# HGRN projections as pairs of channel tiles over both token halves, with the residual stream held in DRAM

## The chip, the cores and the metric

The kernel runs on one core of one Trainium2 chip. The metric is device time in microseconds (us), the median of several executions. A core has TensorE (PE in the profile, with PEld for its weight loads), VectorE (DVE), ScalarE (ACT), GpSimd (POOL) and SyncE (SP), which issues all of this kernel's DMAs.

## The reference, cut to what matters

A trunk of two layers over 1024 tokens of width 1024. Each layer is a token mixer and a gated convolutional FFN, each after an RMS norm with a shift and a scale, each added to the residual stream x. Layer 0 mixes with a chunked gMLP, layer 1 with HGRN2, a gated linear recurrence:

```python
q, fz, i, g = jnp.split(h @ w_in, 4, axis=-1)      # four projections, 1024 x 1024 each
f = lb + (1.0 - lb) * jax.nn.sigmoid(fz)
k = 1.0 - f
q = jax.nn.silu(q)
o = hgrn2_chunked_scan(q, k, i, log(f))            # 8 heads of 128 channels
o = o * lax.rsqrt(jnp.mean(o * o, axis=-1, keepdims=True) + EPS) * gn_g
return (o * jax.nn.silu(g)) @ w_out
```

Everything is float32. A product of two float32 matrices is made of three matmuls in a reduced float32 format: each operand is split into a high part and the remainder (low part), and high x high, high x low and low x high are summed (mm3, L268 to L272).

## The kernel before, in words

x is held transposed in SBUF (xT: 128 partitions, 8 channel tiles, 1024 tokens), and all work goes by two token halves of 512, LO and HI. Operations are not issued as they are written: each is given to a planner (class Plan) with its engine, an assumed duration, what it reads and writes and a priority `pr`; the planner schedules them by list scheduling, in its model port=True steps of DVE and POOL exclude each other, and the order that it finds is then the order of the program on each engine.

Both up projections of the FFN, and the gMLP's, use `class Pairs`. A pair is two channel tiles of weights (r = 0, 1) times two halves of tokens. It is computed as a 2 x 2 block product with the weights' channels split in an upper and a lower half of k-tiles (TOP and the rest), in seven products where the plain form has eight. Per pair, `pair` forms four sums of weight blocks (p_comb, L480), splits seven weight operands (p_split: the high half on ACT, L470; the low half on DVE or POOL, L473), runs seven products of 4 k-tiles x 3 matmuls of 512 columns, copies three products from PSUM (snap, ACT, L698) and adds four (add, DVE, L701). The token side needs operands that are made once: `combos` builds, per k-tile of TOP, the sums of the four blocks of h and splits them into T1, T2, T3 and T4 (L646 for the shifted sums). `plain_pair` computes a pair in eight products.

The HGRN stage of layer 1 follows the first FFN. Its norm (p_sum, p_stats, ln_p) gives h in high and low parts for each half, first LO, then HI, whose last steps come behind the down projection's last products; the scaled x of the norm goes to a ring of tiles (tring). Then 16 units, head by half (u = 2 x head + half):

- `project`: three projections (f, q, g) of one head for one half, each 8 k-tiles x 3 matmuls of 512 columns (h_proj, weights stationary), then the gates: sigmoid and scale on ACT, 1 - f (L1434), the silu products (L1444, L1451) and the product with f (L1446) on DVE.
- `iproj`: the values i, token tiles stationary, for two heads at a time: 4 x 8 tiles x 8 k-tiles x 3 matmuls of 256 columns. So the values come out by token and need no transpose.
- `scan`: seven levels (1, 2, ... 64 tokens). Each level multiplies keys and queries (L1487), multiplies halves of keys, queries and decays by decays on DVE (L1493, L1514), copies the others on ACT (L1497) and puts masked scores into place (L1470, L1531). Then the keys are transposed (L1549), the state is updated (L1556, L1565, L1567), the output computed (L1576, L1578), normalised (L1582, the root, L1590) and transposed (L1598), multiplied with the gate (L1600) and stored to DRAM as operands of the output projection (store, L1619).

Weights of a head come as 1024-wide tiles by DMA (L484), are split by ACT and POOL (h_weight), and each unit's projections are written next to the scan of the unit before.

The output projection (block_out) runs seven block products P1, P2, P6, P7, P4, P5, P3 over the stored operands and adds into xT (p_evac, L412). P1 needs only the first halves of the even heads, P2 the first halves of the odd heads, P6 and later products everything. Its weights and operands are loaded and split as buffers come free (L473 with n as output). The second FFN follows with two plain pairs, its combos and twenty pairs.

Of the kernel before, what the change touches and what calls it, by code (L numbers as in the profile page):

```python
# [7 lines left out]
F32 = mybir.dt.float32  # L8
F32R = mybir.dt.float32r
# [4 lines left out]
P = 128  # L14
# [224 lines left out]
def trunk(tc, a, pool, psum, dram):  # L239
# [20 lines left out]
    acts = dram.tile([NPAIR // 2, 7, P, HT], F32, name="act")  # L260
    hacts = dram.tile([NH // 2, 7, P, HT], F32, name="hact")
# [108 lines left out]
    def bv(i, o=0, n=512):  # L370
        return View(bankl[i], o, n)
# [232 lines left out]
    class Pairs:  # L604
# [32 lines left out]
        def combos(self, k, pr, t1=None):  # L637
# [15 lines left out]
            for i, (n, t) in enumerate((("T2", a22), ("T1", s1), ("T3", a12), ("T4", a21))):  # L653
                if n != "T1" or t1 is None:
                    p_split(pl, t, *self.b[n][k], "V", pr + 0.1 * i)

        def product(self, j, i, slot, fine):
            _, bn, bank_, more = self.PRODUCTS[i]
            pl, pr = self.pl, self.base + 7 * j + i
            ps = bv((4 * j + self.b0 + bank_) % 8)  # L660
# [12 lines left out]
        def pair(self, j, fine=False):  # L673
# [3 lines left out]
            def p(i):  # L677
                return self.base + 7 * j + i
# [640 lines left out]
    tring = Seq(*(v for c in nc_[0:2] for v in two(c, F32)))  # L1319
# [38 lines left out]
    hcell = [hc[i] for i in (6, 0, 3, 5, 8, 1, 11, 10, 4, 7, 9, 2)]  # L1358
    sigs = Seq(*parts(hcell[0], 512, 512))
    f_a, f_b = parts(hcell[1], 512, 512)  # L1360
    q1, k1 = parts(hcell[2], 512, 512)
    qx, = parts(hcell[3], 768)
    sc_a, = parts(hcell[4], 512)
    fs = Seq(f_a)
    scs = Seq(sc_a, f_b)
    sgs = Seq(*parts(hcell[5], 512, 512))
    vts = Seq(*(parts(hcell[i], 1024)[0] for i in (6, 7, 8)))
    ots = Seq(*parts(hcell[9], 512, 512))
    gos = Seq(*(v for i in (10, 11) for v in parts(hcell[i], 512, 512)))
    t23 = rv(2, 0, 512), rv(2, 512, 512)  # L1370
    pjs, lvs, mis = Seq(0, 1, 2), Seq(3, 4), Seq(5, 6, 7)
    lbc, omc = lbt[:, 3 * KT:4 * KT], lbt[:, 4 * KT:5 * KT]
    p_load(pl, masks, a["masks"], HB - 20)
    hw, vtok, gout = {}, {}, {}

    def h_weight(key, src, pr):
        x = wraw.next()
        hw[key] = hi, lo = wsets.next()
        p_load(pl, x, src, pr)
        p_split(pl, x, hi, lo, "G", pr)  # L1380
# [3 lines left out]

    def iproj(m, tb, pr):
        hf = tb // 4
        if tb % 4 == 0:
            vtok[m, hf] = vts.next()
        b, vt = bv(mis.next(), 0, 256), sub(vtok[m, hf], tb % 4 * 256, 256)
        ts_ = slice(tb * P, tb * P + P)  # L1390
        for q in range(2):
            ws = hw["i", m, q]
            xs = [hop2(4 * q + k, ts_) for k in range(4)]

            def fn(ws=ws, xs=xs, q=q):
                hi, lo = (w.r.rearrange("p (k f) -> p k f", f=256) for w in ws)
                for k, (xh, xl) in enumerate(xs):
                    mm3(b.f, (xh.r, xl.r), (hi[:, k, :], lo[:, k, :]), q == 0 and k == 0, q == 1 and k == 3)
            pl.op("PE", 1.45, fn, r=(*ws, *(v for x in xs for v in x)), w=(b,), pr=pr)
        pl.op("S", 0.4, lambda: S.activation(vt.f, b.f, AF.Copy), r=(b,), w=(vt,), pr=pr)  # L1400

    def h_proj(u, n, pr):
        h, hs = u // 2, halves[u % 2]
        hi, lo = hw[n, h]
        b = bv(pjs.next())
        for k0 in range(0, KT, 2):
            xs = [hop2(k, hs) for k in (k0, k0 + 1)]

            def fn(k0=k0, xs=xs):
                for k, (xh, xl) in enumerate(xs, k0):  # L1410
                    c = slice(k * P, (k + 1) * P)
                    mm3(b.f, (hi.r[:, c], lo.r[:, c]), (xh.r, xl.r), k == 0, k == KT - 1)
            pl.op("PE", 1.362, fn, r=(hi, lo, *(v for x in xs for v in x)), w=(b,), pr=pr)
        return b

    class Unit:
# [3 lines left out]
        def project(self, pr):  # L1420
            h = self.h

            def op(eng, dur, fn, r, w, port=False):
                pl.op(eng, dur, fn, r=r, w=w, pr=pr, port=port)

            def gate(b):
                s_ = sigs.next()
                op("S", 0.6, lambda: S.activation(s_.f, b.f, AF.Sigmoid), (b,), (s_,))
                return s_
            s_ = gate(h_proj(self.u, "f", pr))  # L1430
            f, kk = fs.next(), k1
            op("S", 0.79, lambda: S.activation(f.f, s_.f, AF.Identity, scale=omc[:, h:h + 1], bias=lbc[:, h:h + 1]),
               (s_,), (f,))
            op("V", 0.43, lambda: V.tensor_scalar(out=kk.f, in0=f.f, scalar1=-1.0, scalar2=1.0, op0=ALU.mult, op1=ALU.add),  # L1434
               (f,), (kk,), True)
            b = h_proj(self.u, "q", pr)
            s_q = gate(b)

# [15 lines left out]
        def scan(self, pr, prev, lvs, mis):

            u, h, hf = self.u, self.h, self.hf
            sc = scs.next()
# [79 lines left out]
            v = vtok[h // 2, hf]  # L1537

            def vc(c):
                o = c * 256 + h % 2 * P  # L1540
                return v.f[:, o:o + P]

            def cs(c):
                return slice(c * P, (c + 1) * P)
# [45 lines left out]
            op("V", 0.7, lambda: V.tensor_tensor(out=o.f.rearrange("p (c f) -> p c f", f=P),  # L1590
                                                 in0=b3.f.rearrange("p (c f) -> p c f", f=P),
                                                 in1=r.unsqueeze(2).to_broadcast([P, 4, P]), op=ALU.mult),
               (b3, ("small1", 0, 16)), (o,))
# [27 lines left out]

    units = [Unit(u) for u in range(nu)]
    prev = None
    for u in range(-1, nu):

        pr = HB + 10 * u + 5
        if u == -1:
            for n in "fqg":
                h_weight((n, 0), a["hg" + n][0], pr - 15)
            for q in range(2):  # L1630
                h_weight(("i", 0, q), a["hgi"][0, q], pr - 12)
        if u >= 0:
            prev = units[u].scan(HB + 10 * u, prev, *((lvs, mis) if u < nu - 2 else (Seq(2, 3),) * 2))
        if u + 1 < nu:
            if u + 1 == nu - 1:
                pjs = Seq(0, 1)
            units[u + 1].project(pr)
        if u == -1:
            for tb in range(8):
                iproj(0, tb, pr + 1 + 10 * (tb // 4))  # L1640
        m = (u + 3) // 4
        if u >= 1 and m < NH // 2:
            i = (u + 3) % 4
            for tb in range(2 * i, 2 * i + 2):
# [11 lines left out]
    held = [v.life.cell for n in "fqg" for v in hw[n, NH - 1]]  # L1656
    free6 = [c for c in wc if c not in held]
# [129 lines left out]
def _lay_out(inp):  # L1787
# [37 lines left out]
    out["hgi"] = hw[:, 2 * D:3 * D].reshape(2, 4, P, 4, 256).transpose(3, 0, 2, 1, 4).reshape(4, 2, P, 1024)  # L1825
# [24 lines left out]
```

## Time and profile before

| | |
|---|---|
| median of 3 runs | 2450.69 us (2450.42 to 2450.77) |
| the profiled execution's own time | 2449.32 us |
| its span, first to last instruction | 2447.5 us |
| PE / PEld busy | 2411.3 / 2025.4 us |
| DVE / ACT / POOL busy | 1987.3 / 1199.3 / 473.3 us |
| granted TensorE clock, mean | 0.996 |

Times in a view are counted from the span's start. A group row has the line, engine, operation, output and inputs by the program's names, the shapes and the count; behind the first bar the busy time and the mean of one in ns, behind the second the idle time of the engine just before, and what ended it. A window row has its bounds and length, then the busy time of each engine (x instructions), the granted clock, the DMA engines' share and GB/s. A timeline row has start, duration, engine, line and operation, and in brackets the idle time before it. A wait row has who waited for whom, the total, the number and the longest. A DMA row has the count, the size and the median time from issue to landing. A matmul's own duration overlaps its neighbours', so rates are taken from runs of many.

### The profile page before, as it was taken

What the parts mean: (1) busy time and instruction counts of PE and PEld (TensorE: products, weight loads), DVE (VectorE), ACT (ScalarE), POOL (GpSimd) and SP (SyncE); (2) the same over time, 40 slices, a digit from 0 to 9 for tenths busy, and PEclk for the clock granted to TensorE, in tenths of its full rate; (3) what the DMA queues carried; (4) which work ended last, traced back from release to release, by engine and by line L of the source; (5) the groups of instructions that cost most, each with busy time, mean ns of one, the idle gap of its engine ahead of it and who ended that gap; (6) DMA issues with size and microseconds to landing.
All of it is one profiled execution on the core that took longest, in us unless ns stands there. A gap on an engine that the chain in (4) does not pass through costs nothing.

```text
span 2447.5 us, 33499 instructions
## 1 busy us (share of the span) xinstructions
PE 2411.3 (99%) x11870; PEld 2025.4 (83%) x11870; DVE 1987.3 (81%) x3176; ACT 1199.3 (49%) x2066; POOL 473.3 (19%) x289
## 2 busy tenths in 40 slices
PE   9999999999999999999999999999999999999998
PEld 7888788888788888888889898888777888888886
DVE  8888988898999888977846565657999989989756
ACT  5324665455555554445534444435455555554444
POOL 0222111222222221013211111100222222220121
PEclk9999999999999999999999999999999999999999
DMA  9897669720333324734111111123302332338333
GB/s 357 278 358 263 205 226 323 240 89 24 124 96 123 114 86 166 247 114 120 47 48 35 65 36 57 44 74 108 99 26 87 121 121 92 107 114 299 95 102 97
DMA packets 156266, 331.99 MB, mean 136 GB/s; under 512 B 15681, under 2 KB 34497, under 8 KB 156098
## 3 DMA queue, kind: packets, MB, share of 16 engines
q1 hardware_dynamic: 156098, 329.86, 40.5%
q8 instruction: 93, 1.52, 0.3%
q14 instruction: 75, 0.61, 0.1%
HBM read 254.82 MB, written 74.97 MB: 135 GB/s over the span
## 4 chain that ended last, share of the span: by engine, by line
PE 91%; DVE 4%; DMA 3%; ACT 1%; issue 1%; SPq 0%; DVEq 0%; ACTq 0%
PE pb L272 84%; PE pb L1487 3%; PE pb L1219 1%; DVE h L473 1%; PE pb L1556 1%; PE pb L1576 1%; PE pb L1578 0%; DMA xT<-vd 0%; DVE h L280 0%; PE pb L343 0%; DVE n L473 0%; DMA h<-in_ada 0%; DVE w L473 0%; PE pb L1549 0%; DMA w<-in_down 0%
## 5 line engine op out<-in xcount | busy, mean ns | idle before, releaser
L272 PE MATMUL pb<-h,w 128*128 128x512 f32 (+1 forms) x4212 | 977.6, 389 | 7.7 <-DVE h L473 2.5
L272 PE MATMUL pb<-n,w 128*128 128x512 f32 x3936 | 951.1, 393 | 8.0 <-DVE n L473 3.4
L272 PEld LDWEIGHTS pb<-h,w 128*128 128x128 f32 x4212 | 785.5, 188 | 175.2 <-DVE h L473 5.0
L272 PEld LDWEIGHTS pb<-n,w 128*128 128x128 f32 x3936 | 729.9, 188 | 160.8 <-DVE n L473 5.4
L473 POOL TENSOR_TENSOR w<-w,w 128x512 fp32r<-128x512 f32 x158 | 249.6, 1586 | 862.6 <-ACT w L470 761.4
L470 ACT ACTIVATE w<-w 128x512 fp32r<-128x512 f32 x384 | 237.1, 627 | 245.8 <-PE pb L272 144.4
L272 PE MATMUL pb<-w,n 128*128 128x512 f32 (+1 forms) x1536 | 272.5, 337 | 3.7 <-DVE n L458 3.4
L856 DVE SCALAR_TENSOR_TENSOR raw<-wk,prm,raw 128x1024 f32<-128x1024 f32 x168 | 267.4, 1602 | 5.4 <-ACT raw L852 4.2
L272 PEld LDWEIGHTS pb<-w,n 128*128 128x128 f32 x1536 | 238.3, 190 | 36.1 <-DVE n L458 3.9
L473 POOL TENSOR_TENSOR w<-raw,w 128x1024 fp32r<-128x1024 f32 (+1 forms) x48 | 115.2, 2409 | 529.0 <-ACT w L470 450.5
L473 DVE TENSOR_TENSOR w<-w,w 128x512 fp32r<-128x512 f32 x226 | 161.2, 718 | 40.1 <-ACT w L470 39.4
L470 ACT ACTIVATE w<-n 128x512 fp32r<-128x512 f32 x136 | 85.9, 632 | 173.3 <-PE pb L272 163.1
L698 ACT ACTIVATE wk<-pb 128x512 f32<-128x512 f32 x160 | 94.7, 593 | 136.6 <-PE pb L272 115.1
L473 DVE TENSOR_TENSOR w<-n,w 128x512 fp32r<-128x512 f32 x136 | 100.8, 744 | 60.1 <-ACT w L470 59.7
L701 DVE TENSOR_TENSOR wk<-pb,wk 128x512 f32<-128x512 f32 x160 | 108.4, 687 | 45.7 <-PE pb L272 41.2
L470 ACT ACTIVATE h<-h 128x512 fp32r<-128x512 f32 x198 | 122.1, 617 | 15.9 <-DVE h L473 5.8
L473 POOL TENSOR_TENSOR h<-h,h 128x512 fp32r<-128x512 f32 x48 | 67.9, 1416 | 256.0 <-ACT h L470 245.1
L852 ACT ACTIVATE raw<-wk,prm 128x1024 f32<-128x1024 f32 x84 | 103.6, 1240 | 26.0 <-DVE raw L480 11.5
L1493 DVE TENSOR_TENSOR wk<-wk 128x256 f32<-128x256 f32 x192 | 98.0, 534 | 21.8 <-PE pb L1487 11.1
L473 DVE TENSOR_TENSOR h<-h,h 128x512 fp32r<-128x512 f32 x150 | 109.4, 732 | 5.0 <-ACT h L470 5.0
L1497 ACT ACTIVATE wk<-wk 128x256 f32<-128x256 f32 x192 | 75.6, 417 | 77.1 <-PE pb L1487 61.9
L280 DVE SCALAR_TENSOR_TENSOR h<-h,raw 128x1024 f32<-128x1024 f32 x81 | 103.5, 1305 | 1.5 <-DMA h<-in_ada 1.5
(221 smaller groups left out, 2414.9 us busy)
## 6 DMA issues: line engine op xcount, KB each, us to landing
w<-in_up SPq DMA_DIRECT2D x88, 512.0 KB, 3.7
h<-in_ada SPq DMA_DIRECT2D x81, 512.0 KB, 5.8
act<-raw SPq DMA_DIRECT2D x154, 256.0 KB, 2.3
h<-act SPq DMA_DIRECT2D x124, 256.0 KB, 2.7
n<-in_down SPq DMA_DIRECT2D x64, 256.0 KB, 5.4
h<-gact SPq DMA_DIRECT2D x56, 256.0 KB, 4.0
gact<-xT SPq DMA_DIRECT2D x52, 256.0 KB, 3.7
vd<-h SPq DMA_DIRECT2D x32, 256.0 KB, 4.5
```

What stands on the lines that cost most here:

```text
L272: PE.matmul(ps, L[i // 2], R[i % 2], start=first and i == 0 and not more, stop=last and i == 2, skip_group_check=more)
L280: V.scalar_tensor_tensor(out=raw, in0=raw, scalar=1.0, in1=condr, op0=ALU.mult, op1=ALU.mult, accum_out=mod[:, m:m + 1])
L470: pl.op("S", 0.2 + 0.43 * w, lambda: S.activation(hi.r, src.f, AF.Copy), r=(src,), w=(hi,), pr=pr)
L473: lambda: e.tensor_tensor(out=lo.r, in0=src.f, in1=hi.f, op=ALU.subtract), *preds,
L698: pl.op("S", 0.6, lambda: S.activation(c.f, ps.f, AF.Copy), r=(ps,), w=(c,), pr=p(i) - 10)
L701: pl.op("V", 0.69, lambda: V.tensor_tensor(out=c.f, in0=ps.f, in1=c.f, op=ALU.add), r=(ps, c), w=(c,), pr=p(i) - 8)
L852: pl.op("S", 1.22, lambda: S.activation(y.f, wk[:, o + PADW:o + PADW + T], AF.Identity, bias=pc("conv_b", l * NUP + b), scale=cw(2)), r=(c ...
L856: pl.op("V", 1.26, lambda w=w: V.scalar_tensor_tensor(out=y.f, in0=wk[:, o + w:o + w + T], scalar=cw(w), in1=y.f, op0=ALU.mult, op1=ALU.ad ...
L1219: PE.matmul(ps.f[:, i * P:(i + 1) * P], v.f[:, i * P:(i + 1) * P], wsT[:, j, :], start=True, stop=True)
L1487: PE.matmul(ps_()[0:m, c, :], K.f[:, c * P:c * P + m], q, start=True, stop=True)
L1493: V.tensor_tensor(out=halves_(X2, s)[:, :, i, :], in0=halves_(X, s)[:, :, i, :], in1=pair2()[:, :, o].unsqueeze(2).to_broadcast([P, 256 // ...
L1497: S.activation(halves_(X2, s)[:, :, i, :], halves_(X, s)[:, :, i, :], AF.Copy)
```

## The change

The f, q, i and g projections go over to Pairs, in a new class HgUp. Pair j = 2 x head holds f and q, pair 2 x head + 1 holds i and g, each for both token halves. The first two pairs are plain (eight products, `plain`), the other fourteen have seven. i now comes out by channel, so `done` transposes it by head and half (four 128 x 128 transposes and a copy). `combos` of the HGRN stage's h runs at unit 0; T1 and T3 are split late, since their places hold h and the plain pairs' weights until then. `prepare` replaces `project`; 1 - f and the scaling of the head's output go to ACT.

The pairs keep seven slots of split weights and four more operands than before, so the residual stream leaves SBUF meanwhile: each block of xT is stored to xspill once it is final, the norm writes its scaled x over it, and during the units xT's place holds values, gates, transposed keys, scores and outputs. At the end 16 loads bring it back. The second half of the norm has all its low parts on DVE, where half of them were on POOL. The cells that the output projection and the second FFN use are those of the first FFN in another order.

The core of the diff:

```diff
+    xspill = dram.tile([P, KT, T], F32, name="xs")
...
-        def combos(self, k, pr, t1=None):
+        def combos(self, k, pr, t1=None, late=()):
...
-                if n != "T1" or t1 is None:
+                if n not in late and (n != "T1" or t1 is None):
...
+    def spill(hf, ds, pr):
+        for d in ds:
+            pl.op("D", 0.73, lambda d=d: nc.sync.dma_start(xspill[:, d, halves[hf]], xT[:, d, halves[hf]]),
+                  r=(xrg(d, halves[hf]),), w=(("xs", 2 * d + hf, 2 * d + hf + 1),), pr=pr)
...
-        ln_p(nms[0], 1, 0, rbv[0], lambda d: tring.next(), lambda d: pr + 20 + d)
+        spill(0, range(KT), pr)
+        ln_p(nms[0], 1, 0, rbv[0], lambda d: xv(d, LO), lambda d: pr + 20 + d)
...
+            spill(1, (d,), at() - 4)
...
-        ln_p(nms[1], 1, 0, rbv[1], lambda d: tring.next(), lambda d: at() + d, "VG")
+        ln_p(nms[1], 1, 0, rbv[1], lambda d: xv(d, HI), lambda d: at() + d)
...
+    sc0, scs = rv(2, 512, 512), Seq(xv(6, HI), xv(7, HI))
+    ots = Seq(xv(4, LO), xv(5, LO))
+    gos = Seq(xv(6, LO), xv(7, LO), xv(2, HI), xv(3, HI))
+    hslots = [fr[9], fr[10], fr[11], hc[7], hc[9], hc[2], hc[8]]
+    vg = [[xv(0, HI), xv(4, HI), xv(1, HI), xv(5, HI)], [xv(d, LO) for d in TOP]]
...
+    class HgUp(Pairs):
+        def __init__(self):
+            self.pl, self.l, self.sub, self.base = pl, 1, 0, HB
+            self.slots = Seq(*(two(c, F32R) for c in hslots))
+            self.early = Seq(*(two(c, F32R) for c in fr[0:8]))
+            self.banks = Seq(0, 1, 2)
+            self.t = {k: ((xv(k, LO), xv(k + 4, LO)), (xv(k, HI), xv(k + 4, HI))) for k in TOP}
+            self.bc = [x for y in zip([hc[1], hc[11], hc[3], fr[8]], fr[4:8], fr[0:4]) for x in y]
+            self.sides()
+        def at(self, j, i):
+            return self.base + 10 * (j - 1) + 1 + i * 9 / 7
+        def bankof(self, j, i):
+            return (0, 1, 0, 1, 0, 1, 0)[i] if j == nu - 1 else (0, 1, 0, 2, 0, 2, 1)[i]
+        def raw(self, j):
+            return rv(0), rv(1), rv(2, 0, 512)
+        def weights(self, j):
+            return [a[("hgf", "hgq", "hgi", "hgg")[2 * (j % 2) + i]][j // 2] for i in range(2)]
+        def done(self, j, r, hf, pr):
+            x, h = self.places(j)[2 * r + hf], j // 2
...
+            elif j % 2 and r == 0:
+                b = bv(mis.next())
+                def fn():
+                    for c in range(4):
+                        PE.transpose(b.f[:, cs(c)], x.f[:, cs(c)], ident)
+                pl.op("PE", 0.5, fn, r=(x,), w=(b,), pr=pr)
+                pl.op("S", 0.6, lambda: S.activation(x.f, b.f, AF.Copy), r=(b,), w=(x,), pr=pr)
...
-            op("V", 0.43, lambda: V.tensor_scalar(out=kk.f, in0=f.f, scalar1=-1.0, scalar2=1.0, op0=ALU.mult, op1=ALU.add),
-               (f,), (kk,), True)
+            op("S", 0.6, lambda: S.activation(k1.f, f.f, AF.Identity, scale=-1.0, bias=ones[:, 0:1]), (f,), (k1,))
...
-            op("V", 0.7, lambda: V.tensor_tensor(out=o.f.rearrange("p (c f) -> p c f", f=P),
-                                                 in0=b3.f.rearrange("p (c f) -> p c f", f=P),
-                                                 in1=r.unsqueeze(2).to_broadcast([P, 4, P]), op=ALU.mult),
-               (b3, ("small1", 0, 16)), (o,))
+            def scaled():
+                for c in range(4):
+                    S.activation(o.f[:, cs(c)], b3.f[:, cs(c)], AF.Copy, scale=r[:, c:c + 1])
+            op("S", 1.3, scaled, (b3, ("small1", 0, 16)), (o,))
...
+    up = HgUp()
+    up.start()
+    up.plain(0, (HB - 15, HB - 5))
     units = [Unit(u) for u in range(nu)]
     prev = None
+    for u in range(nu):
+        units[u].prepare(HB + 10 * u - 5)
+        if u == 0:
+            for k in TOP:
+                up.combos(k, HB + 1 + 0.5 * k, late=("T1", "T3"))
+            up.plain(1, (HB - 14, HB + 5))
+            for n, i in (("T1", 0), ("T3", 1)):
+                for k in TOP:
+                    p_split(pl, up.t[k][i][0], *up.b[n][k], "V", HB + 3 + 0.5 * k)
+        if u and u % 2 == 0:
+            up.pair(u + 1)
+        prev = units[u].scan(HB + 10 * u, prev, *((lvs, mis) if u < nu - 2 else (Seq(2, 3),) * 2))
+        if u % 2 and u + 1 < nu:
+            up.pair(u + 1)
+    for hf, ds in ((0, TOP), (1, range(KT)), (0, range(4, KT))):
+        for d in ds:
+            p_load(pl, xv(d, halves[hf]), xspill[:, d, halves[hf]], HB + 10 * nu - 1, r=(("xs", 2 * d + hf, 2 * d + hf + 1),))
...
-    held = [v.life.cell for n in "fqg" for v in hw[n, NH - 1]]
-    free6 = [c for c in wc if c not in held]
+    free6, held = [fr[i] for i in (8, 11, 7, 4, 5, 6)], [fr[i] for i in (0, 1, 2, 3, 9, 10)]
```

More of the change, by code (lines that the diff above doesn't have):

```diff
@@ L1318, in trunk, with xv @@
     nc_ = bc[10:11] + bc[2::3]
-    tring = Seq(*(v for c in nc_[0:2] for v in two(c, F32)))
+    xf = xT.rearrange("p k t -> p (k t)")
+    xl = Life("x", KT * T, ap=xf)
+    def xv(d, hs):
+        return View(xl, d * T + hs.start, HT)
+    def spill(hf, ds, pr):
+        for d in ds:
+            pl.op("D", 0.73, lambda d=d: nc.sync.dma_start(xspill[:, d, halves[hf]], xT[:, d, halves[hf]]),
+                  r=(xrg(d, halves[hf]),), w=(("xs", 2 * d + hf, 2 * d + hf + 1),), pr=pr)
     sqs2 = Seq(*two(nc_[2], F32))
@@ L1370, in trunk @@
-    t23 = rv(2, 0, 512), rv(2, 512, 512)
-    pjs, lvs, mis = Seq(0, 1, 2), Seq(3, 4), Seq(5, 6, 7)
+    fr = f0.freed
+    fqp = [parts(hc[i], 512, 512) for i in (10, 4)]
+    sigs = Seq(*parts(hc[0], 512, 512))
+    q1, k1 = parts(hc[6], 512, 512)
+    qx, = parts(hc[5], 768)
+    sc0, scs = rv(2, 512, 512), Seq(xv(6, HI), xv(7, HI))
+    ots = Seq(xv(4, LO), xv(5, LO))
+    gos = Seq(xv(6, LO), xv(7, LO), xv(2, HI), xv(3, HI))
+    hslots = [fr[9], fr[10], fr[11], hc[7], hc[9], hc[2], hc[8]]
@@ L1372, in trunk, with vgs @@
+    vg = [[xv(0, HI), xv(4, HI), xv(1, HI), xv(5, HI)], [xv(d, LO) for d in TOP]]
+    (v0, g0), vg7 = parts(hslots[6], 512, 512), [v for c in hslots[0:2] for v in parts(c, 512, 512)]
+    def vgs(h):
+        return [v0, vg[0][1], g0, vg[0][3]] if h == 0 else vg7 if h == NH - 1 else vg[h % 2]
+    lvs, mis = Seq(3, 4), Seq(5, 6, 7)
     lbc, omc = lbt[:, 3 * KT:4 * KT], lbt[:, 4 * KT:5 * KT]
     p_load(pl, masks, a["masks"], HB - 20)
[L1374 to L1380, printed above, removed]
+    gout = {}
@@ new lines, in cs, with at, bankof, places @@
+    def cs(c):
+        return slice(c * P, (c + 1) * P)
+    class HgUp(Pairs):
[7 more added lines that the diff above has]
+            self.sides()
+        def at(self, j, i):
+            return self.base + 10 * (j - 1) + 1 + i * 9 / 7
+        def bankof(self, j, i):
+            return (0, 1, 0, 1, 0, 1, 0)[i] if j == nu - 1 else (0, 1, 0, 2, 0, 2, 1)[i]
[3 more added lines that the diff above has]
+            return [a[("hgf", "hgq", "hgi", "hgg")[2 * (j % 2) + i]][j // 2] for i in range(2)]
+        def places(self, j):
+            return vgs(j // 2) if j % 2 else [*fqp[0], *fqp[1]]
+        def done(self, j, r, hf, pr):
+            x, h = self.places(j)[2 * r + hf], j // 2
+            if j % 2 == 0 and r == 0:
+                pl.op("S", 0.6, lambda: S.activation(x.f, x.f, AF.Sigmoid), r=(x,), w=(x,), pr=pr)
+                pl.op("S", 0.79, lambda: S.activation(x.f, x.f, AF.Identity, scale=omc[:, h:h + 1], bias=lbc[:, h:h + 1]),
+                      r=(x,), w=(x,), pr=pr)
+            elif j % 2 and r == 0:
[5 more added lines that the diff above has]
+                pl.op("S", 0.6, lambda: S.activation(x.f, b.f, AF.Copy), r=(b,), w=(x,), pr=pr)
+            elif j % 2:
+                s_ = sigs.next()
+                pl.op("S", 0.6, lambda: S.activation(s_.f, x.f, AF.Sigmoid), r=(x,), w=(s_,), pr=pr)
+                pl.op("V", 0.7, lambda: V.tensor_tensor(out=x.f, in0=x.f, in1=s_.f, op=ALU.mult), r=(x, s_), w=(x,),
+                      pr=pr, port=True)
+        def plain(self, j, prs):
+            for x, w in zip(self.raw(j), self.weights(j)):
+                p_load(pl, x, w, prs[0] - 15)
+            ws = {}
+            for r in range(2):
+                for c in range(2):
+                    ws[r, c] = self.early.next()
+                    p_split(pl, rv(r, 512 * c, 512), *ws[r, c], "G", prs[0] - 15)
+            for hf, hs in enumerate(halves):
+                for r in range(2):
+                    b, c_ = bv(self.banks.next()), self.places(j)[2 * r + hf]
+                    for k0 in range(0, KT, 2):
+                        hi, lo = ws[r, k0 // 4]
+                        xs = [hop2(k, hs) for k in (k0, k0 + 1)]
+                        def fn(k0=k0, hi=hi, lo=lo, xs=xs, b=b):
+                            for k, (xh, xl) in enumerate(xs, k0):
+                                c = slice(k % 4 * P, (k % 4 + 1) * P)
+                                mm3(b.f, (hi.r[:, c], lo.r[:, c]), (xh.r, xl.r), k == 0, k == KT - 1)
+                        pl.op("PE", 1.362, fn, r=(hi, lo, *(v for x in xs for v in x)), w=(b,), pr=prs[hf])
+                    pl.op("S", 0.6, lambda c_=c_, b=b: S.activation(c_.f, b.f, AF.Copy), r=(b,), w=(c_,), pr=prs[hf] - 10)
+                    self.done(j, r, hf, prs[hf])
@@ L1382, in sub @@
     def sub(v, o, n):
         return View(v.life, v.o + o, n)
[L1385 to L1414, printed above, removed]
@@ L1535, in scan @@
                 K, Q, T_ = K2, Q2, T2
-            v = vtok[h // 2, hf]
+            v = self.v
             def vc(c):
[L1540 to L1544, printed above, removed]
+                return v.f[:, cs(c)]
             b1, kT = bv(mis.next()), ots.next()
@@ L1824, in _lay_out @@
     out["hgq"], out["hgf"], out["hgg"] = stat(hw[:, 0:D]), stat(hw[:, D:2 * D]), stat(hw[:, 3 * D:])
[L1825 removed]
+    out["hgi"] = stat(hw[:, 2 * D:3 * D])
     out["ho"] = f["hg_w_out"][0].reshape(NH, P, D)
```

87 lines of the change are left out of this document (18 added, 69 removed).

## The prediction

> **What bounds the kernel now.** I read the page first, then one line's summary to get the length of the stage that is changed, then busy times by window, then the groups by line for prices.
>
> ```profile
> span 2447.5 us, 33499 instructions
> PE 2411.3 (99%) x11870; PEld 2025.4 (83%) x11870; DVE 1987.3 (81%) x3176; ACT 1199.3 (49%) x2066; POOL 473.3 (19%) x289
> PE   9999999999999999999999999999999999999998
> DVE  8888988898999888977846565657999989989756
> PE 91%; DVE 4%; DMA 3%; ACT 1%; issue 1%; SPq 0%; DVEq 0%; ACTq 0%
> ```
>
> TensorE is busy in every slice and holds 91% of the chain that ended last. VectorE (DVE) has room in one place, the slices with 4 to 6 tenths: the HGRN stage, the only one that the change touches.
>
> ```profile
> L1487 PE MATMUL pb<-h,h x128: 216/275/276, 1224.7 to 1699.2; 128*128 128x64 f32 x128
> ```
>
> These are the first matmuls of each of the 16 scan units (head by token half). Their first and last starts give the period: (1699.2 - 1224.7) / 15 = 31.64 us a unit.
>
> ```profile
> core 0: us, PE busy (x) PEld busy (x) DVE busy (x) ACT busy (x) POOL busy (x), PEclk, DMA share, GB/s
> 757.00:975.00 218.00, 218.00 (x963) 180.60 (x962) 194.52 (x223) 112.45 (x162) 50.09 (x32) 1.00 0.35 118
> 1224.70:1240.00 15.30, 15.30 (x100) 13.44 (x99) 7.90 (x20) 7.32 (x17) 1.35 (x1) 1.00 0.01 2
> 1240.00:1256.30 16.30, 16.30 (x111) 15.09 (x111) 2.94 (x6) 4.48 (x8) 6.00 (x3) 1.00 0.31 98
> 1256.30:1667.60 411.30, 410.62 (x2698) 367.42 (x2697) 253.07 (x655) 172.86 (x371) 55.64 (x23) 1.00 0.15 50
> 1699.20:1730.00 30.80, 30.64 (x178) 25.71 (x178) 28.38 (x62) 12.76 (x28) 1.29 (x1) 1.00 0.46 151
> 1699.20:1745.00 45.80, 43.50 (x233) 36.07 (x233) 42.48 (x81) 19.54 (x39) 8.99 (x6) 1.00 0.45 139
> ```
>
> The long row is 13 units: PE 410.62 of 411.30 us, so the stage is bound by PE; per unit DVE works 253.07/13 = 19.5 us (idle 12.2), ACT 13.3, POOL 4.3. The first row is the FFN's up projection, which already works in the form the change brings here (pairs, seven products): PE without a gap, with DVE at 194.52/218 = 89%. The granted clock is 1.00 in each of these rows.
>
> **PE: what the change saves.**
>
> ```profile
> 1149.79 45.04 PE L272 MATMUL pb<-h,w 128*128 128x512 f32 x198
> 1213.17 11.68 PE L272 MATMUL pb<-w,n 128*128 128x256 f32 x96
> L272 PE MATMUL pb<-w,n 128*128 128x256 f32 x768 | 96.2, 284 | 0.0
> L1549 PE MATMUL pb<-prm,wk 128*128 128x128 f32 x64 | 9.7, 274 | 0.7 <-DVE wk L1493 0.7
> ```
>
> Back to back a 512-wide matmul takes 45.04/198 = 0.2275 us, a 256-wide one 11.68/96 = 0.1217 us. Removed: the f, q and g projections, 16 units x 3 x 8 k-tiles x 3 = 1152 matmuls, 262.1 us, and the 768 narrow ones of the i projection, 93.5 us; together 355.6. Added: two plain pairs of 96 and fourteen pairs of 7 products x 4 k-tiles x 3 = 84, so 192 + 1176 = 1368 matmuls, 311.2 us; and 16 groups of four transposes for the values, which are of the kind of L1549 (16 groups, 9.7 us). PE loses 355.6 - 320.9 = 34.7 us of work. By unit: 72 x 0.2275 + 48 x 0.1217 = 22.2 us before, 84 x 0.2275 + 0.6 = 19.7 after, so the period that PE allows falls from 31.64 to 29.1 us.
>
> [...]
>
> **DVE, ACT and POOL: what the pairs cost.**
>
> ```profile
> L480 DVE TENSOR_TENSOR w<-w,w 128x512 f32<-128x512 f32 x96 | 72.4, 756 | 0.9 <-DMA w<-in_down 0.7
> L473 DVE TENSOR_TENSOR w<-w,w 128x512 fp32r<-128x512 f32 x226 | 161.2, 718 | 40.1 <-ACT w L470 39.4
> L701 DVE TENSOR_TENSOR wk<-pb,wk 128x512 f32<-128x512 f32 x160 | 108.4, 687 | 45.7 <-PE pb L272 41.2
> L1434 DVE TENSOR_SCALAR h<-h 128x512 f32<-128x512 f32 x16 | 6.7, 421 | 13.3 <-ACT h L1432 13.3
> L1590 DVE TENSOR_TENSOR h<-pb,small 128x512 f32<-128x512 f32 x16 | 10.9, 682 | 0.0
> L473 POOL TENSOR_TENSOR w<-w,w 128x512 fp32r<-128x512 f32 x158 | 249.6, 1586 | 862.6 <-ACT w L470 761.4
> L470 ACT ACTIVATE w<-w 128x512 fp32r<-128x512 f32 x384 | 237.1, 627 | 245.8 <-PE pb L272 144.4
> L646 DVE SCALAR_TENSOR_TENSOR h<-h,mod,h 128x512 f32<-128x512 f32 x12 | 9.9, 828 | 0.0
> ```
>
> One pair per unit puts on DVE four block sums, four low halves and four additions from PSUM: 4 x 0.756 + 4 x 0.718 + 4 x 0.687 = 8.6 us. Two DVE steps of each unit go to ACT (1 - f, and the scaling of the output): 0.421 + 0.682 = 1.1 us off. DVE has 19.5 + 8.6 - 1.1 = 27.0 us a unit, 93% of 29.1. POOL's three splits make 3 x 1.586 = 4.8 us where it had 4.3. ACT gets seven high halves, three snapshots, the value copy, 1 - f and four short scalings; at 0.627 us for each, and with nothing taken off for what leaves, that is 16 x 0.627 = 10.0, so 23.3 us at most, which is no bound.
>
> Does a scan, which is a chain between DVE, PE and ACT, let DVE be filled to 93%? The window 1699.2 to 1730.0 is the last unit with the next stage's work beside it: DVE is busy 28.38 of 30.80 us, idle 2.4. With that idle time the unit takes 27.0 + 2.4 = 29.4 us, 0.3 over PE's 29.1: **14 x 0.3 = 4 us given back**. Bounds: nothing, if DVE keeps ahead of PE, and the 3.3 us of idle time that DVE has per 30.3 us in the FFN window, which is a rival below. Below nothing is excluded, for PE's count is fixed.
>
> **The start.** Both token halves must be there in full before T2, T3, T4 can be built: per k-tile one block sum, three shifted sums and four low halves, 4 x (0.756 + 3 x 0.828 + 4 x 0.718) = 24.4 us of DVE that was not there, and the four low halves of the second norm that leave POOL (at most 4 x 0.83 = 3.3 us, as the shifted sums, which are of their kind). With the first pair's 4 x 0.756 + 4 x 0.718 = 5.9 that is 33.6 us. Cover: in the two windows from 1224.7 to 1256.3 DVE has 31.6 - 7.90 - 2.94 = 20.8 us idle. Up to 13 us of DVE are left over. PE meanwhile has the second half of both plain pairs (96 x 0.2275 = 21.8 us), products 1 and 2 of the first pair, and the first scan. The FFN has the same changeover from plain pairs to pairs twice:
>
> ```profile
> 600.00:640.00 40.00, 37.95 (x165) 30.46 (x164) 35.38 (x47) 20.31 (x31) 11.83 (x7) 1.00 0.30 99
> 1766.00:1810.00 44.00, 41.48 (x185) 33.02 (x184) 40.55 (x74) 21.05 (x34) 10.85 (x5) 1.00 0.11 36
> 1810.00:1862.00 52.00, 48.34 (x202) 38.17 (x200) 50.01 (x60) 31.31 (x48) 14.80 (x7) 0.97 0.12 39
> ```
>
> PE is idle 2.0 us in the first, 2.5 + 3.7 = 6.2 in the second. I take their mean, **4 us**, with 0 and 13 as ends; a gain is excluded, since PE had no idle time there.
>
> **Holding x in DRAM and getting it back.**
>
> ```profile
> act<-raw SPq DMA_DIRECT2D x154, 256.0 KB, 2.3
> h<-act SPq DMA_DIRECT2D x124, 256.0 KB, 2.7
> gact<-xT SPq DMA_DIRECT2D x52, 256.0 KB, 3.7
> 1194.88 0.75 DVE L412 SCALAR_TENSOR_TENSOR xT<-pb,mod,xT 128x512 f32<-128x512 f32 x1 [1.26 <-PE pb L272]
> 1206.74 1.12 PE L343 MATMUL pb<-h,ones 128*128 128x512 f32 x2
> 1734.33 32.71 PE L272 MATMUL pb<-n,n 128*128 128x512 f32 x143 [2.13 <-DVE n L473]
> ```
>
> The 16 spills go out by SP and land in about 3.7 us; the norm's scaled x, which now overwrites x, waits for them. For the first half the last two products of the down projection hide that; for the second, the last block of x is added at 1194.88 and the broadcast that the norm needs starts at 1206.74, 11.9 us later. I cost it at nothing; without that cover it is 3.7 us, and behind the waiting DVE step would stand the whole second-half norm. On SP the spills stand among the weight loads, which wait until POOL's splits free the raw buffers: one such split, 1.6 us, is the price if a spill is caught behind one, and the cover holds that too.
>
> The 16 reloads stand on SP at the end. Most places are free a unit or more early. x[2] and x[3] of the second half hold the last heads' outputs: after the last combination a store (2.3) and a load (about 2.7) must land before product P2 of the output projection can be added into x, and the addition stands in DVE's queue ahead of the splits for P6. Product P1 has a second new wait: its weights are loaded where T3 lay, and its operand buffers are the first half's h, so it can begin only after the last pair; before, it filled the last scan's gaps. Then the scaling on ACT lengthens the last chain by about 1 us. At present PE loses 45.80 - 43.50 = 2.3 us from 1699.2 to 1745, nearly all in the 2.13 of the row above. I take **3 us**; ends are -1, for a part of those 2.3 could be filled, and 10, the store and the load twice over, when DVE stands still for both.
>
> **The sum** against the profiled execution (2449.32 us, of which the span is 2447.5): -34.7 + 4 + 4 + 3 = -23.7, so 2425.6; the median of the runs shown is 1.4 above that execution: **2427.0 us**. Its own range is 2415 (nothing given back in the unit or at the start, -1 at the end) to 2436 (start 8, end 6, units 6).
>
> **The rivals.**
> - DVE cannot be filled beyond the FFN's 89%. Then the unit takes 27.0/0.892 = 30.3 us, 1.2 over PE's: 14 x 1.2 = 16 in place of 4, and the total is -34.7 + 16 + 7 = -12, **2439**. For it: PE and DVE here wait for each other at each of seven levels, in the FFN hardly. Against it: the 92% of the window at 1699.2.
> - The seams cost their upper ends: 13 at the start, 10 at the end, units 4: -34.7 + 27 = -8, **2443**. For it: 33.6 us of new DVE work against 20.8 idle. Against it: both FFN changeovers, which had DVE at 88 to 96% and lost 2 to 6.
> - The other side: the scan's waits stay, and the pairs come on top of them. DVE's steps start in the program's order; where an addition waits for its product, the scan step behind it waits too, and where a scan step waits for PE, so does the split behind it.
>
> ```profile
> DVE h L1470 <- PE pb L1487: 45.8, 26, 5.3
> DVE small L1582 <- ACT h L1580: 22.0, 13, 3.4
> ```
>
>   These waits in the 13 units are a part of DVE's 12.2 us of idle time a unit. It decides at 31.64 - 27.0 = 4.6 us: if more than that stays, the unit is longer than before. If half stays, 6.1, the unit takes 33.1 us: -34.7 + 14 x (33.1 - 29.1) + 7 = +28, **2479**. Against it: the idle time is there because DVE had nothing else, and it fell to 2.4 where it had.
>
>   [...] No row here shows a ready step held behind a waiting one.
>
> **How the numbers follow.** The forecast gets 0.60, DVE at 89% 0.17, the seams 0.10, the scan's waits 0.13. Range 2414 to 2448: it takes in the first three with a little of their spread and leaves out the last. A difference under 0.2% (4.9 us) can hardly be told from none by measurement. Faster: 0.60 + 0.12 + 0.07 = 0.79; within 0.2%: 0.05 + 0.03 = 0.08; slower 0.13.
>
> **What would show it.** The period between the first level's matmuls should be 29.1 to 29.7 us from the third unit on, with DVE at 90 to 93% and PE gapless; 30.3 speaks for the first rival, over 31.6 for the last. PE's idle time between the last product of the first FFN and the third unit should be 0 to 8 us, and from the last scan to the output projection's third product 2 to 6, its releasers DVE's splits. Matmuls of 256 columns should be gone from the stage, and L272 should have some 550 fewer entries. I am wrong if PE has gaps inside the units, or if the reloads of x release them.

## The result, and the profile after

The changed kernel takes 2423.11 us (median of 4 runs, 2420.90 to 2426.61) against 2450.73 for the kernel before: ratio 0.9886, 95% interval 0.9874 to 0.9899, 27.6 us less. The forecast was 2427.0. The profiled execution took 2421.17 us.

From the page of the changed kernel, the lines that answer to those shown of before:

```profile
span 2419.0 us, 33014 instructions
PE 2379.4 (98%) x11382; PEld 1980.1 (82%) x11382; DVE 2066.9 (85%) x3349; ACT 1284.6 (53%) x2280; POOL 462.2 (19%) x303
DVE  8878988898998898976798888888899988989756
PE 91%; DVE 4%; DMA 3%; ACT 1%; issue 1%; SPq 0%; DVEq 0%; ACTq 0%
```

PE has 488 entries fewer: 552 matmuls of the projections gone, 64 transposes come. The valley in DVE's row is gone; the HGRN stage now stands at 8 tenths like the rest.

From the source view of the first level's matmuls, the start of each of the 16 units:

```profile
L1531 PE MATMUL pb<-h,h x128: 217/275/275, 1229.5 to 1666.9; 128*128 128x64 f32 x128
```

The period is (1666.9 - 1229.5)/15 = 29.16 us, where it was 31.64. (The last start in such a row is that of the last of the unit's eight matmuls; from first matmul to first matmul both periods are 0.05 us shorter.) The windows: 13 units, and the stage as a whole, from the first FFN's last product to the sums of the second FFN's first half. Behind them is the same stretch of the kernel before.

```profile
core 0: us, PE busy (x) PEld busy (x) DVE busy (x) ACT busy (x) POOL busy (x), PEclk, DMA share, GB/s
1283.00:1660.00 377.00, 376.92 (x2289) 326.66 (x2288) 312.76 (x774) 240.48 (x541) 51.41 (x38) 1.00 0.22 70
1192.99:1739.52 546.53, 537.03 (x3113) 460.06 (x3113) 460.50 (x1066) 335.07 (x732) 78.74 (x55) 0.99 0.23 73
```

```profile
1194.83:1766.87 572.04, 568.99 (x3599) 503.59 (x3598) 376.13 (x895) 250.24 (x522) 93.34 (x46) 1.00 0.19 62
```

The stage is 25.5 us shorter: PE's busy time falls by 32.0, its idle time rises from 3.1 to 9.5. (The parts ahead of it and behind it are 1.8 and 1.2 us shorter in this pair of executions. Their program hardly changed, and runs of one kernel lie up to 8 us apart (8.1 in one of the experiments, 5.7 here), so I don't read that as an effect.) Inside the units PE is gapless. Where it stands idle is read from its timeline (start, duration, operation; in brackets the idle time before it):

```profile
1207.16 8.47 PE L273 MATMUL pb<-n,w 128*128 128x512 f32 x36 [1.43 <-ACT h L1468]
1689.66 0.73 PE L273 MATMUL pb<-n,n 128*128 128x512 f32 x2 [2.70 <-DVE n L474]
1702.07 0.69 PE L273 MATMUL pb<-n,n 128*128 128x512 f32 x1 [3.59 <-ACT n L471]
1703.87 35.81 PE L273 MATMUL pb<-n,n 128*128 128x512 f32 x146 [1.12 <-DVE n L474]
```

1.4 us at the start of the stage; nearly all the rest at its end, where the output projection waits for its split operands: 2.70 us before the transposes of the last head's output, 3.59 and 1.12 us behind them, before product P6. The last row shows something else: 146 matmuls in 35.81 us are 0.245 us each, where the same product took 32.71/143 = 0.229 before. The clock explains it:

```profile
1695.00:1700.00 5.00, 3.48 (x15) 2.36 (x13) 5.00 (x12) 3.34 (x6) 3.57 (x1) 1.00 0.90 263
1700.00:1705.00 5.00, 1.81 (x4) 1.13 (x5) 3.87 (x4) 0.63 (x1) 3.27 (x3) 0.72 0.90 312
1705.00:1710.00 5.00, 5.00 (x15) 3.93 (x14) 3.02 (x5) 1.03 (x2) 0.32 (x1) 0.60 0.70 215
1710.00:1715.00 5.00, 5.00 (x23) 4.13 (x23) 4.46 (x6) 1.67 (x4) 0.97 (x1) 1.00 0.28 70
```

Behind the gap the granted clock is 0.72, then 0.60, and 15 matmuls start in 5 us in place of 23. 146 x (0.245 - 0.229) = 2.4 us.

### The profile page after: what moved, and what is told of

Same layout as the page of the kernel before. It is cut to its first block, busy times and chain, and to the rows that moved or that the text cites. A ratio compares the mean times of both kernels' runs of the same rounds, so it can differ in the third digit from the quotient of the medians.

```text
span 2419.0 us, 33014 instructions
## 1 busy us (share of the span) xinstructions
PE 2379.4 (98%) x11382; PEld 1980.1 (82%) x11382; DVE 2066.9 (85%) x3349; ACT 1284.6 (53%) x2280; POOL 462.2 (19%) x303
## 4 chain that ended last, share of the span: by engine, by line
PE 91%; DVE 4%; DMA 3%; ACT 1%; issue 1%; SPq 0%; DVEq 0%; ACTq 0%
PE pb L273 83%; PE pb L1531 4%; PE pb L1227 1%; DVE h L474 1%; DVE n L474 1%; DMA w<-in_down 1%; PE pb L1596 1%; PE pb L1616 1%; PE pb L1618 0%; DMA h<-act 0%; DVE h L281 0%; PE pb L1589 0%; PE pb L344 0%; DMA w<-in_ho 0%; PE pb L1438 0%
## 5 line engine op out<-in xcount | busy, mean ns | idle before, releaser
L273 PE MATMUL pb<-h,w 128*128 128x512 f32 (+1 forms) x4338 | 1008.2, 388 | 6.3 <-ACT wk L706 1.7
L273 PEld LDWEIGHTS pb<-h,w 128*128 128x128 f32 x4338 | 807.6, 188 | 178.2 <-DVE h L474 4.5
L273 PE MATMUL pb<-n,w 128*128 128x512 f32 x3312 | 791.4, 392 | 7.1 <-DVE n L474 2.9
L273 PEld LDWEIGHTS pb<-n,w 128*128 128x128 f32 x3312 | 616.9, 188 | 139.6 <-DVE n L474 4.9
L273 PE MATMUL pb<-w,n 128*128 128x512 f32 x768 | 177.8, 393 | 4.1 <-DVE n L459 3.6
L273 PEld LDWEIGHTS pb<-w,n 128*128 128x128 f32 x768 | 145.1, 189 | 35.9 <-DVE n L459 4.0
L474 POOL TENSOR_TENSOR w<-raw,w 128x512 fp32r<-128x512 f32 (+1 forms) x52 | 88.1, 1706 | 402.6 <-ACT w L471 202.5
L413 DVE SCALAR_TENSOR_TENSOR xT<-pb,mod,xT 128x512 f32<-128x512 f32 (+1 forms) x120 | 83.1, 729 | 24.7 <-PE pb L273 23.7
L273 PE MATMUL pb<-n,n 128*128 128x512 f32 x336 | 84.4, 406 | 7.7 <-DVE n L474 4.1
```

What stands on the lines that cost most here:

```text
L273: PE.matmul(ps, L[i // 2], R[i % 2], start=first and i == 0 and not more, stop=last and i == 2, skip_group_check=more)
L413: V.scalar_tensor_tensor(out=xT[:, d, hs], in0=ps.f, scalar=gate(d), in1=xT[:, d, hs], op0=ALU.mult, op1=ALU.add)
L474: lambda: e.tensor_tensor(out=lo.r, in0=src.f, in1=hi.f, op=ALU.subtract), *preds,
```

## The experiments

The theory, from the prediction: PE binds the units, so the time follows the number of matmuls. Rivals: the gain comes from other parts of the rewrite; DVE is the next bound and close; the loss at the end of the stage comes from fetching x back. Three runs of the changed kernel itself serve as yardsticks: 2423.11 above, and two beside the experiments.

> The changed kernel once more, as the yardstick for this chip: 2421 to 2427, with the same idle time of TensorE (1.4 us at the start of the stage, about 8 at its end).

Measured: 2423.50 (2421.86 to 2424.66), ratio to the kernel before 0.9883 (0.9868 to 0.9898).

> The changed kernel beside these two on the same chip: 2421 to 2426, clock at 0.60 to 0.75 for some 8 us behind the gap at the end of the stage.

Measured: 2420.66 (2418.97 to 2425.71), 0.9884 (0.9867 to 0.99). The clock behind the gap was lower for a shorter time than expected: 0.90 and 0.76 in two stretches of 5 us, shown below. Differences under some 4 us between two variants are not told apart here by time; the traces have to do it.

**Eight products in place of seven**

```diff
         if u and u % 2 == 0:
-            up.pair(u + 1)
+            up.plain(u + 1, (HB + 10 * u + 1, HB + 10 * u + 5.5))
...
-            for k in TOP:
-                up.combos(k, HB + 1 + 0.5 * k, late=("T1", "T3"))
```

and the same for the other pairs; T1 and T3 are not made.

> The changed kernel with all sixteen pairs in the plain form (eight products), no combos. Theory 'count' (TensorE binds the units, and the time follows the number of its matmuls): 14 x 12 = 168 matmuls of 0.2275 us come back, 38 us over the changed kernel's 2423, so 2455 to 2463, 3.5 us of TensorE work more than in the kernel before. Rival 'form' (the gain comes from the other things that the rewrite does: i with 512 columns in place of 256, gates and scaling on ScalarE, weights split in halves): it stays below 2440. The unit's period should be 31.9 us by 'count'.

Measured: 2458.63 us, 1.0028 times the kernel before (1.0016 to 1.004), 35.1 over the changed kernel beside it. Its unit starts and its 13 units:

```profile
L1531 PE MATMUL pb<-h,h x128: 217/275/275, 1230.6 to 1708.8; 128*128 128x64 f32 x128
1283.00:1660.00 377.00, 377.00 (x2233) 325.45 (x2232) 199.74 (x564) 199.09 (x450) 60.14 (x46) 1.00 0.17 55
```

The period is 478.2/15 = 31.88 us: 2.72 more than with seven products, and 12 matmuls at 0.2275 are 2.73. So the gain in the units is the product left out, all of it. Everything else in the rewrite together costs about 7 us (2458.63 against 2451.85): 3.5 of added PE work, as counted beforehand, and idle time at the end, here 5.9 us before P6.

**More work for DVE**

In `pair`, for the HGRN stage alone, after each p_split of the slots 2 to 5 on DVE, once or twice:

```diff
+            pl.op("V", 0.68, lambda: V.tensor_tensor(out=lo.r, in0=src.f, in1=hi.f, op=ALU.subtract), r=(src, hi),
+                  w=(lo,), pr=pr, port=True)
```

> The four low halves that VectorE makes for each pair of the HGRN stage are each made twice, the second time over the first with the same values: 4 x 0.6 = 2.4 us more VectorE work a unit, from 24.1 to about 26.5 of 29.1 us, 91%. Theory 'count': no change, 2423 with 3 either way, period 29.1. Rival 'ceiling' (VectorE can't be filled beyond the 89% of the FFN stage): period 26.5/0.892 = 29.7, 14 x 0.6 = 8 us more, 2431.

Measured: 2437.03, 0.9939 (0.9922 to 0.9956), 13.5 us over the changed kernel.

```profile
L1545 PE MATMUL pb<-h,h x128: 217/275/421, 1229.9 to 1682.1; 128*128 128x64 f32 x128
1283.00:1660.00 377.00, 370.37 (x2207) 318.28 (x2206) 326.89 (x793) 230.16 (x521) 47.47 (x36) 1.00 0.19 61
```

> The same, each made three times: 4.8 us more a unit, about 28.9 of 29.1 us, 99%. Theory 'count' with VectorE as the next bound close behind: period about 29.5 to 30.5, 2428 to 2443. Rival 'ceiling': 28.9/0.892 = 32.4, 14 x 3.3 = 46 us more, 2469.

Measured: 2454.42, 1.0012 (1.0003 to 1.0022), 30.9 over it: the whole gain is gone.

```profile
L1545 PE MATMUL pb<-h,h x128: 217/275/323, 1229.9 to 1697.4; 128*128 128x64 f32 x128
1283.00:1660.00 377.00, 361.46 (x2130) 306.58 (x2130) 341.82 (x807) 219.19 (x494) 48.35 (x36) 1.00 0.16 52
```

The period goes from 29.16 to 30.15 to 31.17 us, DVE's busy share from 83% to 87% to 91%, and PE's from 100% to 98.2% to 95.9%. "No change" was wrong for the first dose, and so was a fixed ceiling at 89%: the first dose costs more than the ceiling would (2437 against 2431), the second less (2454 against 2469) and fills DVE to 91%. What holds is softer. A dose, planned at 2.4 us, adds about 2.0 us a unit to DVE's busy time (busy share times period: 24.2, 26.1 and 28.3 us). It costs 1.0 us of the period; the other half is found in DVE's idle time, which shrinks from 4.9 us a unit to 4.0 and 2.9. Whether the delay of the products did it, or the full queue, was left open by these two, so a third put the work where no product waits for it:

```diff
-            op("V", 0.75, lambda: V.scalar_tensor_tensor(out=go.f, in0=b4.f, scalar=pc("gn_g", h), in1=sg.f,
-                                                         op0=ALU.mult, op1=ALU.mult), (b4, sg), (go,))
+            for _ in range(5 if u < nu - 2 else 1):
+                op("V", 0.75, lambda: V.scalar_tensor_tensor(out=go.f, in0=b4.f, scalar=pc("gn_g", h), in1=sg.f,
+                                                             op0=ALU.mult, op1=ALU.mult), (b4, sg), (go,))
```

> Each unit's last step, the product with the gate (0.75 us, its result goes to memory and to a store only), is made five times over in the first fourteen units: four steps of about 0.65 us, 2.6 us more VectorE work a unit, as much as the doubled low halves, but with nothing of TensorE's behind it. 'Occupancy' (the doubled low halves cost 13.5 us because VectorE's queue is nearly full, whatever stands in it): 2433 to 2440, period about 30.1. 'Chain' (they cost it because the second low half delays the product that needs it): 2421 to 2427, period 29.2 with VectorE at 91 to 92%.

Measured: 2436.01, 0.9934 (0.9917 to 0.995), 12.5 over the second yardstick (2423.50).

```profile
L1531 PE MATMUL pb<-h,h x128: 217/275/323, 1227.4 to 1673.8; 128*128 128x64 f32 x128
1283.00:1660.00 377.00, 371.87 (x2236) 320.47 (x2236) 326.36 (x798) 232.22 (x530) 46.52 (x36) 1.00 0.19 64
```

The same share of DVE (87%), nearly the same time, and none of PE's waits in the 13 units ends at an added step: a fuller queue costs PE time by itself. That it explains the whole cost of the doubled low halves is not shown, for the 12.5 us lie elsewhere. The period is 29.76 here, 9.0 us over the 15 periods, where the doubled low halves cost some 14; without the last period, which is 4 to 5 us longer in both, it is 5.1 against 9.5 (from first matmul to first matmul). The rest is lost behind the last unit's start, which comes 759.6 us before the span's end, in the three yardsticks 752.1 to 752.7. So occupancy accounts for a little over half of the cost in the units; the other part may be the delay of the products.

**Holding x in DRAM**

The kernel before, with the spills, the norm that writes over x, and the reloads (those of eight blocks tied to the last head's output):

```diff
+        spill(0, range(KT), pr)
-        ln_p(nms[0], 1, 0, rbv[0], lambda d: tring.next(), lambda d: pr + 20 + d)
+        ln_p(nms[0], 1, 0, rbv[0], lambda d: xv(d, LO), lambda d: pr + 20 + d)
...
+            after = (gout[1, 1],) if (hf == 1 and d in (2, 3, 6, 7)) or (hf == 0 and d > 3) else ()
+            p_load(pl, xv(d, halves[hf]), xspill[:, d, halves[hf]], HB + 10 * nu - 1,
+                   r=(("xs", 2 * d + hf, 2 * d + hf + 1), *after))
```

> The kernel before with only x's part of the change: x is stored to memory block by block, the norm writes its scaled x over it, and 16 loads bring it back, those of eight blocks only after the last head's output. The projections are as before. Both theories of the main gain: no change within 4 us of the kernel before (2448 to 2454). If holding x in memory has a price of its own (3.7 us a stall at the start, 5 at the end), 2455 to 2460.

Measured: 2452.21 (2447.74 to 2454.54), 0.9997 (0.9988 to 1.0007). Holding x in DRAM costs nothing that can be measured. The other way round, the changed kernel without its sixteen loads:

> The changed kernel without the sixteen loads that bring x back at the end of the HGRN stage; the output projection adds to whatever stands in x's place, so the result is not the reference's. 'Reload' (the idle time of TensorE at the end of the stage, 8.0 us against 2.3 before, comes from waiting for x): it falls to 2 to 4 us and the time to 2416 to 2420. 'Backlog' (it comes from VectorE, which is full there with the last scan and the output projection's splits and sums): the idle time stays at 6 to 8 us, 2421 to 2427.

Measured: 2422.15 (2421.75 to 2422.69), 0.9876 (0.9862 to 0.9891), 1.4 us under the second yardstick, within the spread. Its list of PE's waits from 1190 to 1760 us (total, times, longest):

```profile
PE pb L273 <- DVE n L474: 4.3, 3, 2.7
PE pb L273 <- ACT n L471: 2.4, 1, 2.4
PE pb L273 <- ACT h L1468: 1.4, 1, 1.4
PE pb L1531 <- ACT h L1554: 0.6, 1, 0.6
```

The gaps at the end are still there, so 'reload' falls as the reason for most of them. A small part is left to it. In both traces the chain of work that leads to P6 goes from DVE's combinations of the last head's outputs through their stores to a load of one of P6's operands from DRAM, and from there to ACT's split. This is the load, in the changed kernel and then in the run without the reloads (start, duration):

```profile
1696.67 4.69 DMA w<-hact
```

```profile
1699.29 2.92 DMA w<-hact
```

It takes 4.45 to 4.99 us in the three yardsticks and 2.92 without the reloads, and P6 starts 11.3 us after the end of the 2.70 us gap, in the yardsticks 12.4 to 12.7. So the reloads hold P6 back by some 1.2 us, by one trace without them, too little to be seen in the time.

**The end of the stage**

```diff
-            p_split(pl, x, *at[i, m], "VG"[i > 2 and m % 2], pr)
+            p_split(pl, x, *at[i, m], "VG"[bool(i > 2 and m % 2 or i == 1 and narrow)], pr)
```

> The changed kernel with the four low halves of the output projection's product P2 (the operand side) on GpSimd in place of VectorE: 4 x 0.6 = 2.4 us less for VectorE at the end of the stage, 4 x 1.4 = 5.6 us more for GpSimd. 'Backlog', if GpSimd's work goes on beside VectorE's: TensorE's idle time at the end falls from 8 to about 6 us, 2419 to 2423. If steps of the two engines with two inputs in SBUF shut each other out there, as the 2.54 us step in the kernel before suggests: no gain or up to 4 us more, 2423 to 2428.

Measured: 2423.39 (2419.54 to 2427.67), 0.9882 (0.9866 to 0.9898): no difference in time. The gap before P6 is 1.59 us, the one of 2.70 stayed. The fair comparison is not the 3.59 us of the first execution: in the other two yardsticks the gap is 2.40 and 2.33 us, because there the granted clock was lower behind the 2.70 us gap (0.81 from 1695 to 1700 in one, 0.66 from 1690 to 1695 in the other) and PE's work up to the next gap took 10.2 to 10.3 us, as in this run, in place of 8.8. So the move takes about 0.8 us off the gap. That is the direction of 'backlog', but no gain shown.

```diff
+    for _ in range(8):
+        pl.op("PE", 0.4, lambda: PE.matmul(bank[3][:, 0:P], ones, ones, start=True, stop=True), r=(onesrg, gout[1, 1]),
+              w=(bv(3),), pr=HB + 10 * nu + 5)
```

> The changed kernel with eight matmuls of ones (128 columns, their result used by nothing) on TensorE behind the last head's output, where TensorE now stands idle for 3.6 and 1.1 us before product P6. 'Clock' (the gap itself lowers the clock that is granted afterwards: 0.72 and 0.60 in the two stretches of 5 us from 1700, where it was 1.00 before): the clock stays above 0.95 there, the first 25 matmuls of P6 take 5.7 us and not 8.1, and the time falls by about 2 us, 2419 to 2423. If the lower clock has another cause: rows as in the changed kernel, 2422 to 2426.

Measured: 2421.75 (2416.51 to 2423.02), 0.9881 (0.9864 to 0.9897). Two windows of this run, then the same two of the changed kernel beside it:

```profile
1700.00:1705.00 5.00, 3.29 (x12) 2.18 (x12) 3.70 (x5) 2.49 (x5) 3.20 (x3) 1.00 0.82 288
1705.00:1710.00 5.00, 4.93 (x22) 4.02 (x23) 4.20 (x7) 2.01 (x4) 1.29 (x1) 1.00 0.60 204
```

```profile
1700.00:1705.00 5.00, 1.66 (x5) 0.88 (x5) 4.80 (x8) 1.78 (x3) 3.91 (x3) 0.90 0.95 298
1705.00:1710.00 5.00, 5.00 (x18) 3.96 (x18) 3.74 (x7) 1.15 (x2) 0.61 (x1) 0.76 0.84 271
```

The filling matmuls leave 1.83 us of the gap, and the clock stays at 1.00; without them it falls to 0.76. It falls so in all five executions that have this end without them (lowest in a stretch of 5 us: 0.60, 0.71 and 0.76 in the three yardsticks, 0.72 in the run without reloads, 0.77 in the one with P2's low halves on GpSimd) and in neither of the two with them (1.00 in every such stretch from 1690 to 1720): the gap is the cause. From the last head's transposes to the sums of the next norm's first half the trace has 46.3 us (1689.54 to 1735.82) in place of 47.6 (1691.47 to 1739.09); the other four executions without the filling matmuls have 47.1 to 49.3. A gain of that size is inside the spread of the times.

> The same with the four low halves of P2 on GpSimd as well. 'Backlog' and 'clock' add: the idle time and the stretch at the lower clock both shrink, 2416 to 2421; otherwise as the run without it.

Measured: 2422.97 (2421.76 to 2424.35), 0.9892 (0.9875 to 0.9908). The gap before P6 is 0.78 us and that stretch 45.2 us here (1693.59 to 1738.82), but the 2416 to 2421 that were expected did not come. No variant beats the changed kernel by more than the spread.

## Why the prediction came out right, point by point

**PE's count: right.** 34.7 us were counted. PE's busy time in the stage fell by 32.0, and 2.4 of the missing 2.7 are the matmuls at the lower clock. The experiment with eight products gave 2.72 us a unit where 2.73 were counted. The 12 matmuls of 512 columns that a unit saves took 2.72 us, 0.227 us each.

**The units: 4 us given back by the forecast, none measured.** Two terms of this step were wrong and offset each other. DVE's load was put at 27.0 us a unit; measured are 312.76/13 = 24.1 in 29.0, 83% where 90 to 93% was the sign to look for. I had added mean durations, and successive steps on DVE overlap. Two successive steps of DVE in the changed kernel's timeline show it:

```profile
1343.71 0.69 DVE L481 TENSOR_TENSOR raw<-raw 128x512 f32<-128x512 f32 x1
1344.31 0.19 DVE L1558 TENSOR_TENSOR wk<-wk 128x32 f32<-128x32 f32 x1
```

A step of 0.69 us occupies 0.60: the next one starts then. Twelve such steps are 7.2 us and not 8.6. And the scan's products on DVE became shorter, by the groups of 13 units before and after:

```profile
L1493 DVE TENSOR_TENSOR wk<-wk 128x256 f32<-128x256 f32 x156 | 82.7, 555 | 13.8 <-PE pb L1487 10.3 <-PE pb L1549 1.0 <-ACT wk L1497 0.7
```

```profile
L1537 DVE TENSOR_TENSOR wk<-wk 128x256 f32<-128x256 f32 x157 | 66.2, 448 | 4.5 <-ACT wk L1541 1.7 <-PE pb L1531 1.0 <-ACT xT L706 0.6
```

82.7 - 66.2 over 13 units is 1.3 us a unit. Before, one such step took 2.54 us (from 1434.18, the group's mean is 0.555) beside a POOL split that took 2.54 us too (from 1433.90); the splits, 1024 wide and 2.42 us on average, are now 512 wide and take 1.39. That this is the reason is argued from the durations, no run tried it. The second wrong term is the claim that DVE can be filled until 2.4 us of idle time are left, without loss to PE. The doses show the loss at 4.0 already. Had the load been the 27.0 that I forecast, this would have cost over 1 us a unit. That the forecast's 4 us and the measured nothing are so near is luck.

**The rival of DVE's ceiling** was wrong as a fixed share, right in its kind: DVE is the next bound, and the change stops just short of it. The rival on the other side, the scan's waits kept in full, is refuted: DVE's idle time fell from 12.2 us a unit to 4.9. That a ready step stands behind a waiting one does occur: in the kernel before, DVE waits 1.80 us for PE before L1567, up to 1407.68, and the L1514 behind it (128x64), whose input was written by 1405.46, starts at 1409.10. The two waits that the prediction quotes for it, 45.8 and 22.0 us in 13 units, are 4.7 (now at L1514) and 1.3 us (L1622). Its point of decision, more than 31.64 us a unit, is where the second dose almost is (31.17), by added work.

**The start: 4 us forecast, 1.4 measured.** The mean of the FFN's two changeovers was too high. The second half's norm and the plain pairs cover each other but for one wait for ACT's copy of a plain product.

**The end: 3 us forecast, about 7.5 measured.** Idle time rose from 3.1 to 9.5 in the whole stage, 5.0 of it beyond the start's 1.4, and 2.4 went to the lower clock. My reason, the reloads, explains little: without them the gaps remain, about 1.2 us shorter. What the sum left out is seen in two windows, from the last unit's first matmul to P6 at full rate, before and after:

```profile
1698.50:1734.33 35.83, 33.53 (x193) 27.91 (x191) 32.70 (x67) 15.94 (x34) 4.97 (x3) 1.00 0.48 153
1666.20:1703.87 37.67, 30.26 (x172) 24.89 (x170) 34.16 (x69) 17.86 (x38) 11.16 (x6) 0.98 0.54 168
```

The stretch is 1.8 us longer, most of it up to the transposes of the last output (24.0 us from 1666.20 to 1690.23, before 22.5 from 1698.51 to 1720.98), and PE has 3.3 us less to do in it: together 5.1 us of idle time. What PE waits for is in part DVE, busy 20.37 of 22.20 us from 1683.8 to 1706 with the last scan, the output projection's splits and its block sums at once. The wait of 2.70 us ends with low halves that stand in DVE's queue behind ten small steps of the last unit's root (1685.93 to 1688.39), while their high halves were ready. The wait before P6 ends with the load and the split named above. Four splits moved to POOL took 0.8 us off that wait, and 1.0 us between the two runs with the filling matmuls. How much of the 5 us a lighter DVE or an earlier load would win back stays open: no run won time there.

Together: -34.7 + 0 + 1.4 + 5.0 + 2.4 = -25.9, measured in the stage -25.5. The forecast had -23.7. Its terms were off by 4 us (units), 2.6 (start) and, the other way, 4.4 (end), so that the total came out nearer than its parts. The median fell by 27.6; what goes beyond the stage's 25.5 lies within the spread of single executions.

## What to carry to other kernels

Where one engine has no gap, count its instructions at the rate of a long run in the trace; that number came true to a few per cent through a rewrite of a whole stage. For the engines that take on the new work, use the spacing of successive steps (0.60 us here) and not the mean duration (0.69), and don't count their idle time as free down to zero: here PE lost nothing with 17% of DVE idle, and 1.0 us of 30 with 13%. The costs that were hard to foresee lay at the stage's end, where two kinds of work meet, and hardly in moving 4 MB out to DRAM and back.

## What the runs showed of the hardware

Gaps of 3.6 and 1.1 us in PE's work were followed by a granted clock of 0.72 and 0.60 over 10 us; with matmuls of no use in the gap, which left 1.83 us of it, the clock stayed at 1.00. So a gap can cost more than its length, here half as much again (2.4 us on 4.7). Its length alone does not decide it. At this place a gap of 2.1 us was followed by a clock of 1.00 in the kernel before (1735 to 1745). The gap of 2.7 us before the last head's transposes was followed by slower matmuls in three of seven executions: the clock was 0.66 from 1690 to 1695 in one yardstick and 0.81 from 1695 to 1700 in another, and in the run with P2's low halves on GpSimd the 33 matmuls behind the transposes took 8.88 us. In the changed kernel's first execution they took 7.89, with a clock of 1.00 from 1690 to 1700.
